# First output projection: operand tiles of the first token block set apart, its left half begun among the last value products, a 2 KB descriptor area

## The chip, the cores and the metric

The kernel runs on one core of a Trainium2 chip. Its time is the device time of one execution in microseconds, as the median of several runs. The trace is one profiled execution of it. The engines are named as in the profile: PE (TensorE, matrix products and transposes), DVE (VectorE), ACT (ScalarE), POOL (GpSimd) and SP (SyncE, which issues most of the DMA transfers).

## What is computed

The reference runs two layers over 1024 tokens of 1024 features in fp32. Layer 0 mixes tokens with a latent attention of 8 heads, layer 1 with a differential attention. Behind each mixer come an output projection, a residual sum with a layer norm, a gated feed-forward part and another such sum. The change sits in layer 0, between the attention and its projection:

```python
o = jnp.einsum('bhqk,bkhd->bqhd', p.astype(v.dtype), v)   # in blocks of 128 queries
o = _from_blocks(o).reshape(b, s, MLA_HEADS * MLA_V)       # 1024 x (8 x 128)
mix = o @ w_o                                              # the output projection
h = _layernorm(ALPHA * h + mix, ln_mix_g[i], ln_mix_b[i])
h = _layernorm(ALPHA * h + _swiglu(h, w_gu, w_down), ln_ffn_g[i], ln_ffn_b[i])
```

## The kernel before

Every fp32 operand of a product is split in two parts, a high one, which ACT casts, and a low one, the rest, which DVE or POOL subtracts. A product of two matrices is then three products on PE: high by high, high by low, low by high. This is `mm3` (L165 to L170).

**Attention.** `attention` (L278) walks over blocks of one head and 128 queries each. The last head goes through its eight blocks in the order 6, 7, 4, 5, 2, 3, 0, 1 (`LAST_ORDER`, L39). A block's scores are made two blocks ahead of its turn; the turn transposes the probabilities on PE and splits them (`transpose_block`, L264 for the high parts, L265 for the low ones). After each pair of blocks `mix_a` sums the values on PE (`pv_group`, L274 and L275, tiles `o_a`), DVE adds the two parts (L1322, tile `ob`), and SP stores the result to DRAM (L1323, `o_dr`). Other work (weights, the next heads' keys) is called in numbered slots between the blocks, by `fill` and `at`.

**Output projection.** `out_proj` (L295) comes after the whole attention. It loads the norm's scale and shift as broadcasts over POOL's queue (`mg`, `mb`, L177) and splits the weights of the 8 heads (`load_w`, L146 and L147, tiles `wo`). Then it takes the token blocks in `LAST_ORDER`. For each it loads the 8 heads' results from DRAM (L319, `of`, 512 KB), splits them in two halves (L323 on ACT, L324 on DVE, tile `oh`), loads the block's input (L330, `zy`, 512 KB, kept behind the load of `of`), and makes a left and a right half of 512 columns by 24 matmuls each (L168 to L170, `zp`). DVE adds the input, `layer_norm` follows, and `raw_x` transposes the block (L173, `xTp`) and copies it (L505, L507) as operand of the feed-forward part `ffn`, whose products `ga`, `gb`, `gc` are at L568.

**What sets the order.** The kernel's text gives the order to a scheduler, which lays out one stream of instructions per engine; each engine then takes its stream strictly in order. `behind` (L182) keeps one instruction after another in that layout without a wait at run time. PSUM tiles come from rotating banks: `banks` opens a set of them, with 2, 3 and 3 banks for the tags s, m and t in attention A (`PS_BUFS_A`) and 4, 2 and 2 afterwards (`PS_BUFS`). A tile that takes a bank waits for those who still use it.

## Time and profile before

| | |
|---|---|
| median of 3 runs | 2262.51 us (2262.24 to 2263.04) |
| profiled execution | 2262.55 us |
| its span, first to last instruction | 2260.8 us |
| mean granted TensorE clock | 0.997 |
| PE busy | 2234.5 us, 10850 matmuls |
| DVE busy | 1591.4 us |
| ACT busy | 1007.2 us |
| POOL busy | 886.2 us |
| DMA traffic | 289.25 MB, mean 128 GB/s |

The profiled execution is 1.75 us longer than its span. A row of a timeline has the start in us, the duration in us, the engine, the line, the operation and the tiles (out from in), shapes and count; in brackets behind it stands how long the engine was idle before it and what ended that. Times of transfers are from the issue to the landing of the last byte.

## The change

A class `FirstBlock` holds the operands of the first token block of the projection (block 6). Its tiles `of_first` and `oh_first` lie in a pool `apart` that nothing else uses. Its load, its split and the first 18 products of its left half (heads 0 to 5, `early`) are called from slots of the last head's attention instead of from `out_proj`, and the weights of heads 0 to 5 too. The remaining products of the left half and the whole right half stay in `out_proj`. The load of the first block's input `zy` is no longer kept behind the load of `of`. The high and low parts of the transposed probabilities that come after the split are kept behind it (`newest["first", ...]`). Attention's set of PSUM banks is kept through the projection; the set of 4, 2 and 2 is opened after it. POOL's descriptor area is 2048 bytes.

```diff
+                for key in ("hi", "lo"):
+                    if ("first", key) in newest:
+                        behind(newest[key], newest.pop(("first", key)))
...
+    class FirstBlock:
+        HEADS = 6
...
+        def load(self):
+            self.of = apart.tile([P, H, P], F32, tag="of", name="of_first")
+            nc.sync.dma_start(self.of, self.source(self.tb))
+            t = apart.tile([P, 2, D], F32R, tag="oh", name="oh_first")
+            self.ot = t.rearrange("p a (h q) -> p a h q", h=H)
+
+        def split(self, hs):
+            oh, ol = self.ot[:, 0, hs], self.ot[:, 1, hs]
+            newest["first", "hi"] = A.copy(oh, self.of[:, hs]).ins
+            newest["first", "lo"] = V.tensor_tensor(ol, self.of[:, hs], f32(oh), ALU.subtract).ins
+
+        def early(self, h0, h1):
+            if h0 == 0:
+                self.m = ps_m("zp_first")
+            product(self.m, self.ot, self.wo, 0, h0, h1)
...
-                    if prev is None:
-                        behind(i.ins, newest["hi"])
-                        behind(j.ins, newest["lo"])
...
-                behind(nc.sync.dma_start(z, x_src[tb * P:(tb + 1) * P, :]).ins, loaded)
+                i = nc.sync.dma_start(z, x_src[tb * P:(tb + 1) * P, :]).ins
+                if prev is not None:
+                    behind(i, loaded)
...
-                    m = (ps_m if nh == 0 else ps_t)(f"zp_{nm}_{nh}")
+                    begun = prev is None and nh == 0
+                    m = first.m if begun else (ps_m if nh == 0 else ps_t)(f"zp_{nm}_{nh}")
...
-                    mm3(m, [(oh[:, h, :], ol[:, h, :], wo[h][0][:, c], wo[h][1][:, c]) for h in range(H)])
+                    product(m, ot, first.wo, nh, first.HEADS if begun else 0, H)
...
+        first = FirstBlock(w_o_a, o_dr[0])
+        for h in range(first.HEADS):
+            at(8 * H - 8 + h // 2, first.weight, h)
+        at(8 * H - 6, first.load)
+        at(8 * H - 3, first.split, slice(0, 4))
+        at(8 * H - 2, first.split, slice(4, 8))
+        at(8 * H - 2, first.early, 0, 3)
+        at(8 * H - 1, first.early, 3, first.HEADS)
         attention(score_a, turn_a, mix_a, fill, 2, (0, 0))
-
-    banks("ps2", PS_BUFS)
...
+    banks("ps2", PS_BUFS)
...
-    nc = bacc.Bacc("TRN2", target_bir_lowering=False, num_devices=1)
+    nc = bacc.Bacc("TRN2", target_bir_lowering=False, num_devices=1, dynamic_dma_scratch_size=2048)
```

On SP's queue at the end of the attention, before: the store of head 7's sums for blocks 6 and 7 (`ob7_3`), then the loads of the projection's first two blocks, each operand ahead of its input.

```order
L1323 DMA o_dr0_3_94<-ob7_3_4224 128x256
L319 DMA of_a0_6_4453<-o_dr0_3_94 128x8x128
L330 DMA zy_a0_6_4460<-in_x 128x1024
L319 DMA of_a0_7_4528<-o_dr0_3_94 128x8x128
L330 DMA zy_a0_7_4535<-in_x 128x1024
L1323 DMA o_dr0_2_93<-ob7_2_4298 128x256
```

And there now:

```order
L1367 DMA o_dr0_3_97<-ob7_3_4247 128x256
L371 DMA zy_a0_6_4478<-in_x 128x1024
L327 DMA of_first_4292<-o_dr0_3_97 128x8x128
L364 DMA of_a0_7_4527<-o_dr0_3_97 128x8x128
L371 DMA zy_a0_7_4534<-in_x 128x1024
L1367 DMA o_dr0_2_96<-ob7_2_4336 128x256
```

The block's input has moved ahead of its operand; the operand still stands behind the store, whose data it reads.

On ACT at the same place, before: the last transposed probabilities (`pt_a7_...`), the last two weights, then the operands of blocks 6 and 7.

```order
L264 CAST pt_a7_2_1_4322<-pt_a7_3_0_4339 128x2x128
L264 CAST pt_a7_0_0_4362<-pt_a7_0_0_4360 128x128
L264 CAST pt_a7_0_0_4362<-pt_a7_1_0_4365 128x2x128
L146 CAST wo0_6_4443<-r_wo0_6_4444 128x1024
L146 CAST wo0_7_4448<-r_wo0_7_4449 128x1024
L323 CAST oh_a0_6_4455<-of_a0_6_4453 128x512 x2
L323 CAST oh_a0_7_4530<-of_a0_7_4528 128x512 x2
```

And there now:

```order
L265 CAST pt_a7_2_1_4360<-pt_a7_3_0_4377 128x2x128
L333 CAST oh_first_4294<-of_first_4292 128x512 x2
L265 CAST pt_a7_0_0_4402<-pt_a7_0_0_4400 128x128
L265 CAST pt_a7_0_0_4402<-pt_a7_1_0_4417 128x2x128
L147 CAST wo0_6_4468<-r_wo0_6_4469 128x1024
L147 CAST wo0_7_4473<-r_wo0_7_4474 128x1024
L367 CAST oh_a0_7_4529<-of_a0_7_4527 128x512 x2
```

The split of the first block has moved ahead of four casts: two of probabilities and two of weights.

On PE, before: the last value products (`o_a7_1`, `o_a7_0`) and the first projection products behind them.

```order
L274 MATMUL o_a7_1_4348<-pt_a7_2_1_4322,vh3_3_3647 128x2x128
L275 MATMUL o_a7_1_4348<-pt_a7_2_1_4322,vl3_3_3648 128x128
L274 MATMUL o_a7_0_4370<-pt_a7_0_0_4362,vh3_0_3415 128x512
L275 MATMUL o_a7_0_4370<-pt_a7_0_0_4362,vl3_0_3416 128x256
L274 MATMUL o_a7_0_4370<-pt_a7_0_0_4362,vh3_1_3476 128x2x128
L275 MATMUL o_a7_0_4370<-pt_a7_0_0_4362,vl3_1_3477 128x128
L168 MATMUL zp_a0_6_0_4463<-wo0_0_4411,oh_a0_6_4455 128x512
L169 MATMUL zp_a0_6_0_4463<-wo0_0_4411,oh_a0_6_4455 128x512
L170 MATMUL zp_a0_6_0_4463<-wo0_0_4411,oh_a0_6_4455 128x512
```

And there now, from the end of `o_a7_1` and again around `o_a7_0` (`zp_first` is the left half, `zp_a0_6_1` the right one):

```order
L278 MATMUL o_a7_1_4388<-pt_a7_2_1_4360,vh3_3_3650 128x2x128
L279 MATMUL o_a7_1_4388<-pt_a7_2_1_4360,vl3_3_3651 128x128
L345 MATMUL zp_first_4407<-wo0_0_4170,oh_first_4294 128x512 x2
L345 MATMUL zp_a0_6_1_4488<-wo0_0_4170,oh_first_4294 128x512 x2
L345 MATMUL zp_first_4407<-wo0_0_4170,oh_first_4294 128x512
...
L345 MATMUL zp_first_4407<-h_wo0_5_4288,oh_first_4294 128x512
L278 MATMUL o_a7_0_4431<-pt_a7_0_0_4402,vh3_0_3418 128x512
L279 MATMUL o_a7_0_4431<-pt_a7_0_0_4402,vl3_0_3419 128x256
L278 MATMUL o_a7_0_4431<-pt_a7_0_0_4402,vh3_1_3479 128x2x128
L279 MATMUL o_a7_0_4431<-pt_a7_0_0_4402,vl3_1_3480 128x128
L345 MATMUL zp_first_4407<-wo0_6_4468,oh_first_4294 128x512
```

Twenty-eight projection products, of both halves, have moved ahead of the four products of `o_a7_0`.

## Rows read from the trace of the kernel before

**Rows 1.** The page: its first line and part 1, busy time of each engine.

```profile
span 2260.8 us, 30078 instructions
...
PE 2234.5 (99%) x10850; PEld 1880.9 (83%) x10850; DVE 1591.4 (70%) x2944; ACT 1007.2 (45%) x2077; POOL 886.2 (39%) x711
```

**Rows 2.** The list of PE's waits: engine, line, releaser; us in total, times, longest.

```profile
PE zp_a L168 <- ACT oh_a L323: 3.8, 1, 3.8
```

**Rows 3.** PE's timeline around the turn (start us, us, ...).

```profile
344.63 0.50 PE L274 MATMUL o_a<-pt_a,vh 128*128 128x512 f32 x1
...
349.19 0.79 PE L168 MATMUL zp_a<-wo,oh_a 128*128 128x512 f32 x1 [3.76 <-ACT oh_a L323]
...
350.99 0.63 PE L168 MATMUL zp_a<-wo,oh_a 128*128 128x512 f32 x1
...
354.67 0.40 PE L168 MATMUL zp_a<-h_wo,oh_a 128*128 128x512 f32 x1
...
359.89 0.39 PE L170 MATMUL zp_a<-wo,oh_a 128*128 128x512 f32 x1
```

**Rows 4.** Windows of 1 us: busy us by engine, then granted clock, DMA share, GB/s.

```profile
347.00:348.00 1.00, 0.00 (x0) 0.00 (x0) 0.00 (x0) 0.00 (x0) 1.00 (x2) 0.81 1.07 396
348.00:349.00 1.00, 0.00 (x0) 0.00 (x0) 0.00 (x0) 0.48 (x1) 1.00 (x1) 0.50 1.04 366
```

**Rows 5.** ACT's timeline at the turn.

```profile
344.01 2.00 ACT L146 CAST wo<-r_wo 128x1024 fp32r<-128x1024 f32 x2
348.52 1.14 ACT L323 CAST oh_a<-of_a 128x512 fp32r<-128x512 f32 x2 [2.51 <-DMA of_a<-o_dr]
```

**Rows 6.** SP's timeline at the turn and at a later block: issues of transfers.

```profile
330.75 8.77 SPq L1323 DMA_DIRECT2D o_dr<-ob  x2
340.93 0.38 SPq L319 DMA_DIRECT2D of_a<-o_dr  x1
341.36 0.58 SPq L330 DMA_DIRECT2D zy_a<-in_x  x1
...
342.72 2.24 SPq L330 DMA_DIRECT2D zy_a<-in_x  x1
...
398.38 0.33 SPq L330 DMA_DIRECT2D zy_a<-in_x  x1
399.73 0.37 SPq L319 DMA_DIRECT2D of_a<-o_dr  x1
```

**Rows 7.** Transfers by issue: KB, us to landing; stretches from 340.5, 341.2, 342.6, 365.2, 399.7.

```profile
of_a<-o_dr SPq DMA_DIRECT2D x1, 512.0 KB, 7.6
...
zy_a<-in_x SPq DMA_DIRECT2D x1, 512.0 KB, 8.4
...
zy_a<-in_x SPq DMA_DIRECT2D x1, 512.0 KB, 9.7
...
of_a<-o_dr SPq DMA_DIRECT2D x1, 512.0 KB, 3.8
...
of_a<-o_dr SPq DMA_DIRECT2D x1, 512.0 KB, 4.4
```

**Rows 8.** POOL's timeline at the turn.

```profile
345.14 4.65 POOL L147 TENSOR_TENSOR wo<-r_wo,wo 128x1024 fp32r<-128x1024 f32 x2 [3.21 <-ACT wo L146]
```

**Rows 9.** Timelines of PE and ACT at the start of the feed-forward part.

```profile
445.16 0.48 PE L568 MATMUL ga<-xh_m,op_gp 128*128 128x512 f32 x1
...
445.44 0.59 ACT L507 COPY xr_m<-xTp_a 128x512 f32<-128x512 f32 x1 [0.96 <-PE xTp_a L173]
...
498.66 0.47 PE L568 MATMUL gb<-t3h_f,op_g 128*128 128x512 f32 x1 [0.67 <-ACT op_g L524]
...
502.42 0.50 PE L568 MATMUL gb<-t4h_f,op_g 128*128 128x512 f32 x1 [0.76 <-DVE tmp L655]
```

**Rows 10.** Timelines of DVE and PE at the last block's transposes.

```profile
449.78 1.28 DVE L206 SCALAR_TENSOR_TENSOR y_a<-y_a,rs_a,mb 128x1024 f32<-128x1024 f32 x1 [0.66 <-POOL rs_a L205]
...
453.42 1.03 PE L173 MATMUL xTp_a<-ident,y_a 128*128 128x128 f32 x8
```

## What I predict, and why

> **What bounds the kernel now.** I first read the page: TensorE (PE) is busy for 2234.5 us of a span of 2260.8 us [rows 1], so only 26.3 us in the whole program are there to be won from waits, and a clock below full speed costs something on top. I then read the list of waits for the longest that lies where the change works: the first product of the output projection waits 3.8 us for the cast of its operand, once [rows 2]; it is the longest single wait that this list shows for PE. The PE timeline around it shows two things. After the last value products (o_a of token blocks 0 and 1, which end 3.76 before the first product of the projection, at 345.43) nothing runs until 349.19; then twelve products start in 354.67 − 349.19 = 5.48 us, while the next 23 start in 359.89 − 354.67 = 5.22 us, 0.227 us each [rows 3]. At 0.227 the first twelve would have taken 2.72 us; 2.76 us are lost. [...] The last nine of the twelve start 0.409 us apart, 0.18 over the full-speed pace; the first three need 1.80 us in place of 1.23, since the third product of a head takes the low halves, which VectorE (DVE) makes behind ACT's cast [rows 3]. So of the 2.76 us some 2.2 belong to the clock and 0.57 to the low halves. In all 3.76 + 2.76 = 6.5 us are at stake at the turn from attention to projection.

> What ends the wait is a chain. ScalarE (ACT) has had nothing to do since 344.01 + 2.00 = 346.01, waits 2.51 us for the load of_a and casts at 348.52 [rows 5]. That load was issued at 340.93 [rows 6], when the store of the last head's sums had landed, and took 7.6 us [rows 7], to 348.5. Neither PE nor the order of ACT decides, but a transfer.

> **The change, part by part.** (1) *The load.* It has a tile of its own now, so no buffer holds it back. But it did not wait for a buffer: it reads what the store of head 7, group 3, has written. DVE's reduction and that store stay where they are, so 340.93 stays. What changes is its neighbour: the input block zy_a, 512 KB, stood behind it on SP's queue (issued 341.36) and now stands ahead, and goes out as soon as the store has been issued, at 330.75 + 8.77 = 339.5 [rows 6]. What that costs has two bounds. At most: before, zy_a landed at 341.36 + 8.4 = 349.8, 1.3 us behind of_a; if the two only change places, of_a lands 1.3 us later. At least: nothing, if zy_a is through in the 1.4 us of lead (that the load itself comes out sooner is the first rival). Between them lies a quieter pair: the load of a later block took 3.8 us alone, and 4.4 where it was issued at 399.73, 1.35 us behind a zy_a [rows 6, 7], nearly the same lead. I take that difference, +0.6, so of_a lands at 349.1 and PE starts at 349.8.

> [...]

> (2) *The earlier start on PE.* The order puts 28 products of the block ahead of the four o_a matmuls of group 0, that were the last before the wait. They wait for the same load through the same cast. PE therefore stops 345.43 − 344.63 = 0.80 us earlier [rows 3] and does these 0.80 us of work later: they no longer lie in front of the wait but behind its end: +0.8. In return the four products that open the block take only high halves, which gives DVE time for the low ones: of the 0.57 I take −0.5. The stop lasts longer than before, so the clock falls as before and its 2.2 us stay: 0.

> (3) *ACT's new order.* The two casts of the block stand ahead of the casts of the last transposed block and of the weights wo0_6 and wo0_7, and ACT takes them in order. So these wait for the load too. The weights' casts took 2.00 us for two [rows 5] and ran while ACT had nothing else to do; now they come after 350.3. PE reaches wo0_6 behind the 28 products and o_a: at 349.8, twelve slow ones end at about 354.7, sixteen more at 0.227 at 358.3. Both high halves are there by about 353. That leaves 5 us for GpSimd's low halves, which took 4.65 us for two [rows 8]: the first is done well ahead, and the second is wanted later. Cost 0; without that cover at most the rest of one low half, 2 us.

> (4) *The 2 KB area and the tiles apart.* The smaller descriptor area could hold GpSimd back between its DMAs; around the turn it issues two, and I see nothing else of its path that PE waits for: 0, bounded by −0.3 (if mb is held and of_first has the engines for longer) and +0.3.

> (5) *The PSUM banks.* The projection keeps the attention's 2, 3 and 3 banks, and the feed-forward's 4, 2 and 2 come after it. Hence the first ga product takes a bank that the transposes ahead of it have just filled, and must wait for ACT's copy out of it. Before, it started at 445.16 without a wait; the copy ran from 445.44 for 0.59 us, to 446.03 [rows 9]: +0.87 at most. The transposes of the last block move ahead by twelve products: from 453.42 to 450.70, plus 0.87 is 451.57, and their input y_a is ready at 449.78 + 1.28 = 451.06 [rows 10], so no wait arises. Further on PE waited 0.67 for ACT and 0.76 for DVE [rows 9]; a PE that comes 0.87 later finds part of this gone. If all is absorbed the net is 0, if nothing, +0.87; the reordered DVE and ACT work there may also take away the two waits, −1.4, at best, with the bank wait hidden. I take +0.3, nearer to the absorbed case. The layer boundary further on is rearranged a little: 0, ±0.3.

> Sum: +0.6 + 0.8 − 0.5 + 0.3 = +1.2 us. On the profiled execution (2262.55; 1.75 of it around the span) this gives 2263.75. The median of the runs is 2262.51, 0.04 lower: 2263.7.

> **The rivals.** *The load lands early* (faster). With the lead of zy_a and no more disturbance than at the later block, of_first lands after 4.4 us, at 345.3, and the first product starts 0.69 behind it as before (349.19 − 348.5), at 346.0. PE would stand still for 346.0 − 344.63 = 1.4 us in place of 3.76, and in the trace the clock was at 0.81 only in the microsecond from 347, 1.6 us after PE stopped; the 2.2 us of the clock and the 0.5 of the low halves go too: −2.4 − 2.2 − 0.5 + 0.3 = −4.8, 2257.7. For it speaks the quiet row; against it, that the two broadcasts stand in GpSimd's order where they stood, so that they are in flight with the load as before, when it took 7.6 us. [...]

> *The load lands last* (slower). Of the four loads that SP issued here the last took 9.7 us from 342.72, to 352.4 [rows 6, 7]. If of_first, behind zy_a and against the broadcasts, comes out there, it is 3.9 us later than before, and with the 0.8, −0.5 and 0.3 the sum is +4.5: 2267.0. It decides from a landing at 352.4 on. Against it: only zy_a has been put ahead, and the bound for that is 1.3.

> *No early start at all.* If the products wait as before and only the order differs, the turn and the banks cancel and the time is 2262.5 ± 1: that differs from the forecast by 1.2 us, but not in its verdict.

> **How the numbers follow.** I call 0.2%, 4.5 us, what a measurement of this kernel can tell from no change. The forecast, with the terms' bounds 2261.0 to 2265.6, has 0.60; no early start 0.17; the early landing 0.14, of which 0.11 lies beyond 0.2% (its gain is about that size, and the bank wait or DVE's order may add a little); the last landing 0.09, of which 0.08 beyond. Faster 0.11, same 0.81, slower 0.08. The range for 8 in 10 reaches to 2258.5, short of the early landing, and to 2266.5.

> **What would show it.** The PE wait ahead of the first product of block 6: about 5.2 us (349.8 − 344.6), for ACT's cast. The load's time from issue to landing: 8.2 us; 4.4 for the first rival, over 11 for the second. [...] The first ga product: a wait of up to 0.9 us for ACT's copy xr. The forecast is wrong if of_first lands before 347, so that the clock doesn't fall, or after 352.

## The result, and the profile after

The changed kernel takes 2266.20 us as the median of 20 runs (2263.95 to 2271.33), the kernel before 2262.97 us (2259.83 to 2266.12). The ratio is 1.0016, with a 95% interval from 1.0010 to 1.0022: the change makes the kernel slower by 2.3 to 5.0 us, most likely by 3.2 to 3.6. I had forecast +1.2 us and called that no change; with 20 runs the measurement told apart less than the 0.2% I had reckoned with.

The profiled execution of the changed kernel took 2266.24 us, 3.69 us more than that of the kernel before. Of these, 2.1 us lie within the span and 1.6 outside it (2266.24 − 2262.9 = 3.3, where the kernel before had 1.75). First the head of its page, with the span and the busy times, to be laid beside [rows 1], then its list of PE's waits (us in total, times, longest):

```profile
span 2262.9 us, 30083 instructions
...
PE 2235.7 (99%) x10850; PEld 1882.4 (83%) x10850; DVE 1595.0 (70%) x2944; ACT 1006.9 (44%) x2077; POOL 889.5 (39%) x711
```

```profile
PE zp_first L345 <- ACT oh_first L333: 5.1, 1, 5.1
...
PE ga L612 <- ACT xr_m L551: 0.7, 1, 0.7
```

The first wait is the one of [rows 2], longer by 1.3 us, and the second is new. PE's timeline around the turn from attention to projection, to be laid beside [rows 3]:

```profile
345.80 0.22 PE L279 MATMUL o_a<-pt_a,vl 128*128 128x128 f32 x1
351.08 1.22 PE L345 MATMUL zp_first<-wo,oh_first 128*128 128x512 f32 x2 [5.05 <-ACT oh_first L333]
352.10 1.05 PE L345 MATMUL zp_a<-wo,oh_first 128*128 128x512 f32 x2
352.95 3.57 PE L345 MATMUL zp_first<-wo,oh_first 128*128 128x512 f32 x10
...
359.53 0.39 PE L278 MATMUL o_a<-pt_a,vh 128*128 128x512 f32 x1
```

The early products stand where they were meant to stand, ahead of the last four of o_a, and wait with them. Next the granted clock in windows of 1 us (the third number from the end), as in [rows 4]:

```profile
348.00:349.00 1.00, 0.00 (x0) 0.00 (x0) 0.00 (x0) 0.00 (x0) 0.00 (x0) 0.77 0.98 270
350.00:351.00 1.00, 0.00 (x0) 0.00 (x0) 0.00 (x0) 0.59 (x2) 0.00 (x0) 0.50 1.13 359
354.00:355.00 1.00, 1.00 (x4) 0.80 (x3) 0.57 (x1) 0.91 (x2) 1.00 (x1) 0.50 0.00 0
355.00:356.00 1.00, 1.00 (x5) 0.79 (x4) 1.00 (x2) 0.00 (x0) 1.00 (x2) 0.82 0.00 0
```

It falls to 0.77 and then 0.50 while PE stands still and is at 0.50 for the first four microseconds of the products (five in the kernel before). The transfers issued in the stretch from 342.0, with KB and the time from issue to landing, answer to [rows 7]:

```profile
mg<-in_ln_mix_g POOLq DMA_DIRECT2D x1, 512.0 KB, 4.9
mb<-in_ln_mix_b POOLq DMA_DIRECT2D x1, 512.0 KB, 7.5
of_first<-o_dr SPq DMA_DIRECT2D x1, 512.0 KB, 8.0
```

The load takes 8.0 us, 0.4 more than before, beside the two broadcasts.

To see where the time went I matched PE's products of the two traces by their tiles and took how late each starts against the kernel before. A single trace carries chance with it, so the same was done for every run below. The delays, in us, at five places (in the kernel before's time), beside each kernel's ratio to the kernel before and its interval:

| kernel | 300 us | 435 | 510 | 960 | 985 | ratio (interval) |
|---|---|---|---|---|---|---|
| changed | 1.48 | 1.86 | 1.64 | 1.64 | 2.71 | 1.0016 (1.0010 to 1.0022) |
| changed, once more | 0.11 | 1.42 | 2.26 | 2.26 | 2.95 | 1.0012 (1.0004 to 1.0021) |
| changed, zy behind | 0.22 | 0.07 | 0.94 | 0.94 | 1.74 | 1.0024 (1.0014 to 1.0035) |
| changed, broadcasts late | 0.10 | −5.47 | −4.63 | −4.62 | −3.77 | 0.9993 (0.9984 to 1.0002) |
| before, banks only | 1.04 | −0.22 | 0.62 | 0.62 | 1.31 | 1.0009 (1.0001 to 1.0018) |
| before, banks only, once more | 1.40 | 0.42 | 1.34 | 1.34 | 2.14 | one run |
| before, area only | 1.75 | 1.27 | 1.29 | 1.29 | 1.04 | 1.0003 (0.9995 to 1.0012) |
| changed, no early products | 0.23 | 3.23 | 3.23 | 3.23 | 3.11 | 1.0022 (1.0013 to 1.0031) |
| before, broadcasts late | 0.21 | −4.55 | −4.53 | −4.53 | −4.57 | 0.9989 (0.9980 to 0.9997) |
| before, late split | 0.19 | −4.15 | −4.14 | −4.14 | −4.32 | 0.9977 (0.9966 to 0.9988) |
| before, late split, once more | 1.16 | −3.17 | −3.15 | −3.15 | −3.16 | 0.9984 (0.9975 to 0.9993) |
| before, split between | 0.39 | −4.37 | −4.33 | −4.33 | −4.38 | 0.9982 (0.9973 to 0.9990) |
| before, idle products | 1.53 | −0.37 | −0.37 | −0.37 | −1.07 | 1.0000 (0.9990 to 1.0010) |

Between 300 and 435 lies the turn, between 435 and 510 the start of the feed-forward part, and before 985 a wait of the down projection. The first column is not the change: it differs by 1.4 us between two traces of the changed kernel, and the kernel before with another area has more of it. Nor is the kernel before's trace, against which all are measured, free of chance.

## The experiments

**The change once more, the area alone, the order of two loads, and the broadcasts.** The first four ran on one chip. The repeated kernel:

> The changed kernel once more, to see what of its trace repeats. Theory A (the turn from attention to projection): the load of the first block takes about 8.0 us again, PE stands still for about 5.05 us, the granted clock falls to 0.50 for 6.83 us. Theory B (the start of the program): the clock rises at 10.6 us instead of 6.3 us again, and PE is 1.5 us late before the turn; if that is chance, the rise comes at another time. Theory C (the start of the feed-forward part): PE waits 0.7 us again for ACT's copy of xr. Time: 1.0010 to 1.0022 of the kernel before.

Its ratio is 1.0012 (1.0004 to 1.0021). The load took 8.3 us and PE stood for 5.36; PE waited 0.7 us for xr again. The clock's first rise came at 4.0 us and not at 10.6, so theory B fell: the 1.5 us that the first trace loses there are chance. In that trace the products at the start are slow for longer: those of 384 columns take 0.52 us there until the clock's rise at 10.6 us and 0.34 behind it, and 0.34 in the kernel before already at 7.1 us. One row from it and one from the kernel before, at the same place of PE's timeline:

```profile
8.48 0.52 PE L1199 MATMUL hq<-wih,xl 128*128 128x384 f32 x1
```

```profile
7.68 0.34 PE L1155 MATMUL hq<-wih,xl 128*128 128x384 f32 x1
```

The area alone:

```diff
-    nc = bacc.Bacc("TRN2", target_bir_lowering=False, num_devices=1)
+    nc = bacc.Bacc("TRN2", target_bir_lowering=False, num_devices=1, dynamic_dma_scratch_size=2048)
```

> The kernel before with nothing changed but the 2 KB descriptor area. If the area delays the start or GpSimd's transfers (theory B), the clock rises at about 10.6 us and the time is 1.5 to 3 us longer, 1.0007 to 1.0013. If the area costs nothing, the ratio is 1.0000 within 0.0004, the load at the turn takes 7.6 us and PE's wait is 3.76 us, as before.

The ratio is 1.0003 (0.9995 to 1.0012); the load took 7.8 us, PE's wait was 4.0. It shows no cost beyond its interval. Its clock rose late too, at 10.5 us, and so did that of the kernel with idle products further below, which has the old area (10.35 us): chance again.

```diff
-                if prev is not None:
-                    behind(i, loaded)
+                behind(i, first.loaded if prev is None else loaded)
```

(`first.loaded` is the load of `of_first`.)

> The changed kernel with the input of the first block kept behind the load of its operand on SP, as before the change. If the input ahead of it delays the load, the load lands after 7.6 instead of 8.0 us or less, PE's wait falls from 5.05 to about 4.6 us, and the time by 0.4 us: too little to be told in the ratio, which stays near 1.0014. Rival: the two transfers share nothing that counts, and the load takes 8.0 us as in the changed kernel.

The load took 7.3 us and PE's wait was 4.42, so the input ahead of the operand costs the load some 0.7 to 1.0 us, between the 0.6 that I took and the bound of 1.3. The turn ends 0.15 us earlier than in the kernel before (0.07 against 0.22), while the two traces of the changed kernel lose 0.38 and 1.31 there. The ratio, 1.0024 (1.0014 to 1.0035), shows no gain from it; its interval overlaps that of the changed kernel.

```diff
-            g = bcast_row(pool, lng, D, "mg0", "g")
-            b = bcast_row(pool, lnb, D, "mb0", "b")
+            g = pool.tile([P, D], F32, tag="g", name="mg0", bufs=1)
+            b = pool.tile([P, D], F32, tag="b", name="mb0", bufs=1)
             for h in range(first.HEADS, H):
                 first.weight(h, ("hi", "scale"), pool)
+            for t, row in ((g, lng), (b, lnb)):
+                behind(nc.gpsimd.dma_start(t, row.partition_broadcast(P)).ins, newest["wlo"])
```

(`newest["wlo"]` is the last low half of a weight on POOL.)

> The changed kernel with the two broadcasts of GpSimd behind the split of the last weight, so that they go out after the load has landed. Theory A (the broadcasts share the DMA engines with the load): the load takes about 4.4 us, as at a later block, PE stands still for about 1.5 us instead of 5.05, the clock stays at 1.00, and some 5.5 us go: about 0.999 of the kernel before, 0.9975 of the changed one. Rival: the load is slow because its packets are small or its source was just written; then it takes 7 to 8 us still, the wait stays near 5 us and the ratio near 1.0014.

Theory A held at the turn. The load landed after 4.0 us; PE's timeline and the load's row in this kernel:

```profile
345.73 0.72 PE L346 MATMUL zp_first<-wo,oh_first 128*128 128x512 f32 x2 [1.08 <-ACT oh_first L334]
346.28 0.63 PE L346 MATMUL zp_a<-wo,oh_first 128*128 128x512 f32 x2
```

```profile
of_first<-o_dr SPq DMA_DIRECT2D x1, 512.0 KB, 4.0
```

PE stands for 1.08 us, the clock stays at 1.00, and the turn ends 5.6 us earlier than in the kernel before (−5.47 against 0.10). It is the first rival's mechanism; its landing time there had been 345.3, and ACT casts at 345.06 here. What the change lacked was not a tile for the load but free DMA engines. From 342 to 345 us, with the load under way in both kernels, the queues' packets, megabytes and shares of the DMA engines' time were these in the kernel before (q0 carries the broadcasts, q1 the transfers that SP issues), and then these in this kernel:

```profile
q0 software_dynamic: 133, 0.48, 61.9%
q1 hardware_dynamic: 485, 0.25, 29.3%
```

```profile
q1 hardware_dynamic: 1448, 0.89, 101.0%
```

In the runs this kernel is 4.0 us faster than the changed one (2262.64 against 2266.68 us), less than the turn's gain in its trace, and 0.9993 (0.9984 to 1.0002) of the kernel before, which is not clear of no change.

**The banks alone, the tiles without the early products.** On a second chip:

```diff
-    banks("ps2", PS_BUFS)
...
     pending = out_proj("left", w_o_a, o_dr[0], x, xs_dr[0], ln_mix_g[0], ln_mix_b[0], xo)
+    banks("ps2", PS_BUFS)
```

> The kernel before, and only the opening of the 4, 2 and 2 PSUM banks moved behind the projection. Theory C (the feed-forward part gives nothing back): PE waits 0.7 us for ACT's copy of xr at the first ga product and 1.3 us at the first product with t3h, in place of 0.67 and 0.76; PE is 0.8 to 0.9 us later from there on, the ratio 1.0004, and the load at the turn takes 7.6 us. Rival (what I predicted): the delay is absorbed in the later waits, net 0.3 us or less.

The ratio is 1.0009 (1.0001 to 1.0018), and theory C held in the trace. PE's waits from 440 to 985 us in this kernel:

```profile
PE gb L568 <- ACT tmp L678: 1.3, 1, 1.3
PE dw L874 <- DVE op_h L524: 1.1, 1, 1.1
PE ga L568 <- ACT xr_m L507: 0.7, 1, 0.7
```

The three waits that the second trace of the changed kernel has in this stretch are here without anything else of the change. From 435 to 510 us PE loses 0.84 us, and 0.69 more before 985. The same kernel once more:

> One more trace of the kernel with only the banks moved: if the loss in the feed-forward part repeats, PE waits 0.7 us for the copy of xr, 1.3 us at the first product with t3h when GpSimd's operation there comes first and DVE's takes 1.5 us (none when GpSimd's takes 1.8 and DVE's 0.7), and 1.0 us near 978 us.

It lost 0.92 and 0.80 us at the two places; PE's waits there were 0.68, 1.35 and 1.21 us, and GpSimd's operation took 1.34, DVE's 1.18. Of the six traces with the banks moved, five lose 0.84 to 0.92 us at the first place, and one (the first of the changed kernel) gains 0.22; all six lose 0.69 to 1.07 before 985. The seven others with the banks as before lose at most 0.04 and nothing there. So the traces pay about 1.5 us on average for the banks.

```diff
-                    begun = prev is None and nh == 0
+                    begun = False
...
-        at(8 * H - 2, first.early, 0, 3)
-        at(8 * H - 1, first.early, 3, first.HEADS)
```

(With the 4, 2 and 2 banks opened ahead of the projection again.)

> The changed kernel without the early products: the first block keeps tiles and load of its own, all its 48 products stay in the projection behind the last value products, and the 4, 2 and 2 banks open ahead of it as in the kernel before. If the early products and the banks carry the loss, PE waits about 4.5 us at the turn (the load still takes 8.0 to 8.3), 0.67 and 0.76 at the feed-forward's gb, and the ratio is 1.0003. If the tiles set apart carry a part through where the other tiles come to lie, the load of rw_t near 965 us still takes 7.0 us or more in place of 6.3, PE's wait at 977 us stays above 1 us, and the ratio is 1.0007.

The losses at 510 and 985 are gone, so the tiles set apart don't carry them. But the turn became worse than in any other kernel:

```profile
352.10 0.80 PE L278 MATMUL o_a<-pt_a,vh 128*128 128x512 f32 x1 [7.31 <-DVE pt_a L266]
```

PE stands 7.31 us, not for the projection's operand but for its last value products: the cast of their probabilities stands behind the load's split on ACT. I had not foreseen this place in the expectation. The turn ends 3.0 us later than in the kernel before (3.23 against 0.23). In the changed kernel 28 products stand ahead of these value products, and PE does not wait for the cast.

**Without the rest of the change.** In the kernel before:

> The kernel before, and only the two broadcasts of GpSimd behind the split of the last weight. Theory A: the load takes 4.0 us instead of 7.6, ACT casts its result as soon as it is done with the weights, at about 346.1 us instead of 348.5, PE waits about 1.3 us instead of 3.76, and the clock stays up: 4.5 to 5 us less, ratio 0.9979. Rival: the gain in the changed kernel needed the early products as well; then PE's wait stays above 2.5 us, the clock falls and the ratio is 0.9993 or more.

The load took 4.0 us, PE waited 0.72 us for ACT's cast and 0.81 for DVE's low half, the clock stayed up (0.999 on average over the profiled execution, 0.997 in the kernel before) and the turn ended 4.76 us earlier: 0.9989 (0.9980 to 0.9997) in the runs, about half of that. The gain does not need the early products. In the next kernel ACT also casts the first block's operand ahead of the last two weights (their casts follow the split and are kept `behind` it):

> As the one before, and ACT casts the first block's operand ahead of the weights of heads 6 and 7. The cast starts when the load has landed, at about 345 us, PE waits about 0.3 us, and 5.5 to 6 us go: ratio 0.9975. If the weights' low halves come too late by it, PE waits for GpSimd near 350 us and the gain is no larger than without this step.

Ratio 0.9977 (0.9966 to 0.9988), 2257.42 us against 2262.82 in the same set. PE's two waits at the turn in this kernel:

```profile
PE zp_a L169 <- POOL wo L337: 1.4, 1, 1.4
PE zp_a L168 <- ACT oh_a L328: 0.4, 1, 0.4
```

The load's wait is almost gone, and GpSimd's low half of the last weight is late in its place, as the expectation had feared: the turn gains 4.34 us in the trace, no more than without this step (4.76). That the ratio came out near the 0.9975 expected is therefore not shown to be this step's doing; its interval overlaps that of the kernel without it. The attempt to remove that too, with head 6 cast ahead of the operand and head 7 behind it, and the first order once more beside it, on a third chip:

> The kernel before with the broadcasts late, and ACT casts the weight of head 6 ahead of the first block's operand and that of head 7 behind it. With the operand ahead of both, PE waited 0.37 us for the operand and 1.40 us for GpSimd's low half of head 7. The cast of head 6 fits into the 1.4 us in which ACT waited for the load, so the second wait should go: about 1.3 us less than that order, 2256 us, ratio 0.9971. Rival: the cast of head 6 ends after the load has landed and delays the operand's; then the first wait grows by up to 0.5 us and the gain is under 1 us.

> The order with the operand ahead of both weights once more, to compare with on the same chip: ratio 0.9977, PE's waits at the turn 0.37 and 1.40 us.

The ratios are 0.9982 (0.9973 to 0.9990) and 0.9984 (0.9975 to 0.9993): no difference. The wait for GpSimd went, and DVE's low half of the operand took its place (PE waited 1.14 us for it): GpSimd's work had started earlier, at 344.83 us instead of 347.20. DVE's low half, 0.69 us long with the operand ahead of both, took 1.84 us beside it. The three orders with late broadcasts in the kernel before beat both kernels, the last two by 0.1 to 0.3%.

**Idle products in the wait, and a packet of instructions.** The load of rw_t, which feeds the product after 975 us, took 7.0 us in the kernel with the banks alone and 6.3 before. In both, one 16 KB packet of the instruction queue falls near it. The queues of two stretches, first in that kernel (967.6 to 968.8 us, within the load), then before (969.7 to 970.8, where the load's last packet lies):

```profile
q1 hardware_dynamic: 180, 0.37, 86.0%
q8 instruction: 1, 0.02, 4.6%
```

```profile
q8 instruction: 1, 0.02, 5.4%
q1 hardware_dynamic: 1, 0.00, 0.1%
```

The kernel before with twelve idle matmuls at the turn, which lengthen PE's stream:

```diff
+                    for _ in range(12 if prev is None and nh == 0 else 0):
+                        T.matmul(m[:, :P], ones, ones, start=True, stop=True)
                     mm3(m, [(oh[:, h, :], ol[:, h, :], wo[h][0][:, c], wo[h][1][:, c]) for h in range(H)])
```

> The kernel before with 12 idle matmuls of 128 columns on PE in the stretch where it waits for the first block's operand (they write a bank that the next product overwrites). Theory D (PE's later wait at 977 us comes from a 16 KB packet of the instruction queue, which falls into the load of rw_t when PE's stream is some 12 matmuls further on): the packet falls about 2.7 us earlier against the products, into the load; the load takes 7.0 to 7.2 us in place of 6.3, PE's wait there is 1.0 to 1.1 us in place of 0.41. Rival: the packet's place has nothing to do with PE's count; then it falls behind the load as before and the wait is 0.4 us or less. The whole time changes by less than 0.04% either way, but for the clock at the turn.

The packet moved, but ahead of the load (959.2 us) and not into it: the load took 6.0 us and PE no longer waited. So in this trace the packet's place went with PE's stream, but the number I expected was wrong. That a packet inside the load is what makes it longer is read from the rows: in all six traces with the banks moved the packet lies inside the load, which takes 7.0 to 7.4 us; in the others it lies at the load's end or ahead of it, and the load takes 6.0 to 6.3. No kernel put the packet into the load with the banks as before. The kernel showed something else, in PE's timeline and the clock's windows:

```profile
346.79 2.89 PE L338 MATMUL zp_a<-ones 128*128 128x128 f32 x24
350.48 0.50 PE L168 MATMUL zp_a<-wo,oh_a 128*128 128x512 f32 x1 [0.80 <-ACT oh_a L323]
```

```profile
348.00:349.00 1.00, 1.00 (x12) 1.00 (x11) 0.00 (x0) 0.00 (x0) 1.00 (x2) 1.00 1.07 359
```

The operand comes 0.2 us sooner behind the last value product, and the clock is still at 1.00 when it comes; the turn ends 1.9 us earlier than in the trace of the kernel before (−0.37 at 435 against 1.53 at 300). The other 1.7 us I put down to the clock, which was at 0.50 in that trace and at 1.00 here. In the runs no gain shows: 1.0000 (0.9990 to 1.0010).

## Why the prediction was wrong

**The turn: right in its rows, less sure in its sum.** I had the load at 8.2 us (8.0 and 8.3), PE's wait at 5.2 (5.05 and 5.36), a clock that falls as before (to 0.50 in both kernels), and +0.9 us in all; the two traces of the changed kernel lose 0.38 and 1.31 there. The bound for zy_a held. The 2.2 us of the clock, which I left unchanged, came from one trace [rows 3, 4], and how much of the products falls into the slow stretch differs from run to run: behind the wait PE runs at a granted clock of 0.50 for 5.3 us in that trace and for 4.3 and 5.6 us in the two of the changed kernel, but for 3.4 us in the trace with the area alone, whose order at the turn is that of the kernel before and which ends the turn 0.48 us earlier. So the turn's loss is known to no better than half a microsecond.

**The casts on ACT: right in the sum, with a price that was too low.** With the early products as cover no wait of PE for these casts shows. Without it I had named at most 2 us, for the weights; in the kernel without early products PE waits for the probabilities' casts behind the split, and the turn ends 3.0 us later than in the kernel before.

**The area: right as far as it can be told**, 0 within an interval of −1.1 to +2.7 us.

**The banks: the step that failed.** "I take +0.3, nearer to the absorbed case" was the wrong choice of the two ends I had. The wait itself came as forecast: 0.68 us for ACT's copy in the kernel with the banks alone, and 0.95 us of delay. Of the two later waits that I had hoped would absorb it, the one of 0.76 us for DVE went, but the one of 0.67 us did not shrink: it grew to 1.3, and 0.84 of the 0.95 stayed. By PE's list it no longer ends with the cast of the operand (L524) but with ACT's L678, which had waited 2.61 us for one of DVE's sums (L653). Just ahead of that sum DVE has another operation (L603), and this one meets one of GpSimd's. Of the two, the one that started second took longer. The rows of GpSimd and DVE in the kernel with the banks alone, then the same two in the changed kernel's first trace:

```profile
496.86 1.29 POOL L524 TENSOR_TENSOR op_g<-s,op_g 128x512 fp32r<-128x512 f32 x1 [47.35 <-ACT op_g L524]
```

```profile
497.44 1.25 DVE L603 TENSOR_TENSOR gr<-gr 128x512 f32<-128x512 f32 x1
```

```profile
498.93 1.79 POOL L568 TENSOR_TENSOR op_g<-s,op_g 128x512 fp32r<-128x512 f32 x1 [47.35 <-ACT op_g L568]
```

```profile
498.87 0.68 DVE L647 TENSOR_TENSOR gr<-gr 128x512 f32<-128x512 f32 x1
```

Where GpSimd started first, DVE's 0.68 us became 1.25 (1.57 in the repeated kernel), DVE ended 1.83 us behind GpSimd's start, PE waited 1.3 us for what follows, and the loss stayed. Where DVE started first, by 0.06 us, it ended 0.62 us behind GpSimd's start, GpSimd's operation took 1.79 in place of 1.29, and PE did not wait there. The difference, 1.21 us, is about PE's wait. That these rows belong together is read from five traces against one; it was not tried by moving the operation. Why the second one takes longer was not shown.

**A term that I did not have.** The 0.7 to 1.1 us before 985 us come with the banks. That they come through the place of an instruction packet against a load fits all traces and was not shown by an experiment. I had looked no further than the layer boundary's order. With this term the banks cost about 1.5 us in the traces where I had put 0.3, which is 1.2 of the 2.0 to 2.4 us by which my sum fell short.

Put together: about 0.4 to 1.3 us at the turn, 0.84 to 0.92 in five of six traces, and 0.7 to 1.1 us, or some 2 to 3.3 us, beside 2.3 to 5.0 measured; the two traces of the changed kernel lose 1.23 and 2.84 us between 300 and 985 us. Another 0.3 us on average lies outside the span, which I had taken for a fixed 1.75 us: nine of the 31 runs of the changed kernel have 2.4 to 3.3 us there, and none of the 93 runs of the kernel before whose span is known has more than 2.2. Why was not tried. The rest is open. PE's waits near 1069, 1392 and 1676 us come and go between traces of kernels that don't differ there (the last is up to 3.1 us long), and the spread of the runs, up to 7 us, is of that size. What moves the instruction packet under the banks alone was not found.

## What to carry to other kernels

A load that ends a wait is not made earlier by giving it a buffer, when its source and its company stay (here 7.6 us before, 8.0 and 8.3 with a tile of its own, 4.0 with the broadcasts late): look first at what else is in flight from any engine's queue, and move that. Before a wait that a reordering adds is counted as absorbed by later ones, look at what ends each of those and whether the reordering delays that as well; until then count it in full. And with changes of a tenth of a per cent, read several traces of each kernel before a term is believed.
